# Reordered GpSimd work, one adding transfer fewer, and first products by two banks in a one-core decoder layer

## The chip, the core and the metric

The kernel runs on one core of a Trainium2 chip. The core has a matrix engine (TensorE; PE in the profile, with PEld for its weight loads), a vector engine (VectorE, DVE), a scalar engine (ScalarE, ACT), GpSimd (POOL), a queue engine that issues most loads (SyncE, SP), and 16 DMA engines. Each engine works off its own list of instructions in order; semaphores order the engines among each other. The metric is the device time of one execution in microseconds (us); less is better.

## What is computed

One layer of a decoder over 288 tokens (256 of a prompt, and 8 requests of 4 new tokens each), 2048 wide:

```python
def trunk_layer(x, hist_conv, hist_pool, pos0, norm1_g, w_in, b_in, conv_w, conv_b,
                ln_g, ln_b, pool_w, pool_scale, w_out, norm2_g, w_ff1, w_ff2):
    h = rmsnorm(x, norm1_g)
    proj = jnp.einsum("btd,de->bte", h, w_in) + b_in
    a, gate, z = proj[..., :D_CONV], proj[..., D_CONV:2 * D_CONV], proj[..., 2 * D_CONV:]
    u = a * jax.nn.sigmoid(gate)
    u_ext = jnp.concatenate([hist_conv, u], axis=1)
    c = jax.nn.silu(layernorm(depthwise_causal_conv(u_ext, conv_w, conv_b), ln_g, ln_b))
    z_ext = jnp.concatenate([hist_pool, z], axis=1)
    d = multiscale_pool(z_ext, pos0)
    p = jnp.einsum("btgc,gce->btge", d, pool_w).reshape(bsz, T, D_POOL) * pool_scale
    mix = jnp.concatenate([c, p], axis=-1)
    x = x + jnp.einsum("btm,md->btd", mix, w_out)
    h2 = rmsnorm(x, norm2_g)
    f = jnp.square(jax.nn.relu(jnp.einsum("btd,df->btf", h2, w_ff1)))
    x = x + jnp.einsum("btf,fd->btd", f, w_ff2)
    return x, u_ext[:, -(CONV_W - 1):], z_ext[:, -(POOL_MAX - 1):]
```

The depthwise convolution has 31 taps; the four pooling groups have windows of 2, 4, 8 and 16. All data are float32. The outputs are the normed x and the new histories.

## The kernel before

**Products in three parts.** A float32 product is made of fp32r ones. Each operand is split into a high half (hi, rounded) and a low half (lo, the rest): `whi`, `wlo` for weights, `hx`, `dx`, `mx`, `ax`, `fx` (each with both halves) for activations. A product is hi x hi, then wlo x hi, then whi x lo, so a pair of 128-row blocks k, k + 1 for one bank of 128 output columns takes six matmuls of 128 x 128 by 288 (`gemm`, all recorded as L291, their order is the list `todo`). A bank is an accumulator of TensorE; `bank2` hands out two of them, from a pool of two such pairs.

**Weights** come in blocks `wr` of 128 x 4 x 256 (512 KB), loaded by SP in the order of `weight_blocks` (two halves for each call of `load`). `split_part` makes `whi` on ScalarE (L260) and `wlo` in one of three ways. V: a subtraction raw - whi on VectorE (L265). G: two subtractions on GpSimd (L268). D: ScalarE writes -whi into `wlo` (L262), and a DMA that GpSimd issues (L263) adds the weights from memory to it; this is called an adding transfer. The table `WAYS` gives the way of each part by stage: "c3": "GDGG" are the four parts of the first loads of convolution pair 3.

**Order of stages.** `SEQUENCE` is c0 c1 c2 c3 c4 p3 c5 p2 P3 c6 p1 P2 p0 P1 c7 P0. c*i* projects the columns of a and gate of 128 convolution channels i (`conv_products`, two banks, 96 matmuls), p*g* those of pooling group g (`pool_group`), P*g* multiplies the pooled d of group g by `pool_w` (`pool_products`, 12 matmuls). p3.1 and so on below means part 1 of the four parts 0 to 3 of a stage's weights. Then w_out (`gemm` on `dx`, the pooled half, eight groups of two banks g = 0 to 7, each followed by an add into `xT` at L579), the layer norm over the convolution's output, w_out again (on `mx`, the convolution's half), and the two matrices of the MLP in a long loop.

**Convolution and pooling.** `conv_pair` multiplies a and gate by the row of norms (L432), builds u (L436), and runs 31 taps over the prompt on VectorE (L448, tile `pc`). For the 8 requests GpSimd multiplies history and taps into `prd` (L451; "history products"), which VectorE sums (L453). The taps are issued with a late priority (`later`), so that they fill what is left of VectorE's time. `pool_group` sums windows on GpSimd (L479 to L483), VectorE makes d of the prompt's columns (L484), and GpSimd d of the requests' columns (L486, L487; "pooling columns").

**TURN.** `classes` reorders the first matmuls of a gemm by the class (k + x) mod 2, where x is 0 for the high half of the activations and 1 for the low. Without it the classes alternate 0, 1, 0, 1; TURN is the string below. It stands at c2, c5, the first gemm of w_out, groups 5 and 7 of the pooled half of w_out, group 2 of its second half, and later in the MLP.

```python
TURN = "110100" * 4 + "01" * 6 + "1100" * 3
WAYS = {"c2": "GVGV", "c3": "GDGG", "c4": "GDGD", "p3": "GDDG", "c5": "GDGD", "c": "GGGV", "p": "GVVG", "w0": "VV", "w": "GG", "ff": "VV"}
```

A scheduler merges the engines' work by program order and priority; `tc.issue_after` forces an instruction behind another one.

## Time and profile before

| what | value |
|---|---|
| time, median of 3 runs | 1082.66 us (1081.39 to 1083.05) |
| the profiled execution's own time | 1082.43 us |
| its span | 1080.6 us |
| TensorE busy | 99% |
| VectorE, ScalarE, GpSimd busy | 59%, 44%, 16% |
| DMA | 190.71 MB, mean 176 GB/s |

The span is what the trace covers; the remaining 1.83 us of the execution lie around it. A row of the timeline gives start and length in us, engine, line, operation, the tiles (out<-in) and their shapes, a count, and in brackets what the first of them waited for. Rows of matmuls overlap, since they are pipelined: the distance of two starts is what a matmul costs. In the lists of waits stand who waited, for whom, the us in total, how often, and the longest. A row of windows has the window, its length, the busy time with the count of instructions, the granted clock, the DMA engines' busy share, and GB/s.

### The profile page before, as it was taken

How to read it: one execution, taken by the hardware profiler on the slowest of the kernel's cores; microseconds unless marked ns; L12 is line 12 of the kernel's file. 1: busy time of each engine (PE TensorE's matmuls, PEld its weight loads, DVE VectorE, ACT ScalarE, POOL GpSimd, SP SyncE). 2: the span in 40 equal slices, each digit the busy share in tenths (PEclk: the TensorE clock that was granted, in tenths of full speed). 3: DMA queues.
4: the chain of work that ended last, by engine and by line, in shares of the span. 5: the costliest groups of instructions: out<-in, count | busy, mean ns of one | idle time of the engine just before them, and what ended most of it. 6: DMA issues, size and time to landing. Idle time of an engine off the chain costs nothing.

```text
span 1080.6 us, 19528 instructions
## 1 busy us (share of the span) xinstructions
PE 1069.2 (99%) x8176; PEld 1067.9 (99%) x8176; DVE 633.7 (59%) x810; ACT 479.0 (44%) x588; POOL 175.9 (16%) x182
## 2 busy tenths in 40 slices
PE   9999999999999999999999999999999999999996
PEld 8999999999999999999999999999999999999996
DVE  7899999788654544444554444555544445554553
ACT  8654445665544433334443333444433334444441
POOL 0878979512000000000000000000000000000001
PEclk9999999999999999999999999999999999999999
DMA  9896478555555555555555555555555555555522
GB/s 326 288 263 182 145 187 247 177 171 173 162 173 166 169 175 163 170 173 165 170 174 164 170 170 167 171 173 162 173 168 167 173 171 164 173 166 170 172 79 88
DMA packets 58296, 190.71 MB, mean 176 GB/s; under 512 B 6240, under 2 KB 11232, under 8 KB 58208
## 3 DMA queue, kind: packets, MB, share of 16 engines
q1 hardware_dynamic: 56336, 184.35, 54.3%
q0 software_dynamic: 1008, 3.67, 1.9%
q8 instruction: 64, 1.05, 0.4%
q10 hardware_dynamic: 864, 1.44, 0.4%
q14 instruction: 24, 0.20, 0.0%
HBM read 185.16 MB, written 4.28 MB: 175 GB/s over the span
## 4 chain that ended last, share of the span: by engine, by line
PE 75%; issue 21%; ACT 2%; POOL 1%; DMA 1%; SPq 0%; POOLq 0%; DVE 0%
PE ac L291 74%; POOL wlo L268 1%; DMA wr<-in_w 1%; ACT whi L349 1%; PE pp L291 1%; DMA wlo<-in_w 1%; ACT hx L354 0%; ACT z_all L405 0%; POOL prd L451 0%; POOL xT L718 0%; ACT whi L260 0%; SPq L191 0%; POOLq L768 0%; DVE xT L691 0%; ACT whi L356 0%
## 5 line engine op out<-in xcount | busy, mean ns | idle before, releaser
L260 ACT CAST whi<-wr 128x1024 fp32r<-128x1024 f32 (+1 forms) x332 | 346.5, 1044 | 551.3 <-PE ac L291 536.7
L265 DVE TENSOR_TENSOR wlo<-wr,whi 128x1024 fp32r<-128x1024 f32 x288 | 353.5, 1227 | 348.1 <-ACT whi L260 348.1
L291 PE MATMUL ac<-ax,whi 128*128 128x288 f32 x2048 | 351.0, 292 | 0.0
L291 PE MATMUL ac<-fx,whi 128*128 128x288 f32 x2048 | 350.2, 292 | 0.0
L291 PEld LDWEIGHTS ac<-ax,whi 128*128 128x128 f32 x2048 | 296.0, 187 | 0.0
L291 PEld LDWEIGHTS ac<-fx,whi 128*128 128x128 f32 x2048 | 295.6, 187 | 0.0
L291 PE MATMUL ac<-ax,wlo 128*128 128x288 f32 x1024 | 217.3, 292 | 0.0
L291 PE MATMUL ac<-fx,wlo 128*128 128x288 f32 x1024 | 216.4, 292 | 0.0
L291 PEld LDWEIGHTS ac<-ax,wlo 128*128 128x128 f32 x1024 | 162.5, 187 | 0.0
L291 PEld LDWEIGHTS ac<-fx,wlo 128*128 128x128 f32 x1024 | 162.2, 187 | 0.0
L291 PE MATMUL ac<-hx,whi 128*128 128x288 f32 x768 | 131.9, 296 | 1.4 <-DVE hx L352 1.4
L718 POOL TENSOR_TENSOR xT<-xT,rf 128x288 f32<-128x288 f32 x4 | 3.1, 795 | 799.9 <-ACT rf L722 799.9
L291 PEld LDWEIGHTS ac<-hx,whi 128*128 128x128 f32 x768 | 112.6, 190 | 1.8 <-ACT hx L354 1.7
L268 POOL TENSOR_TENSOR wlo<-wr,whi 128x512 fp32r<-128x512 f32 x74 | 102.4, 1433 | 17.1 <-ACT whi L260 16.0
L448 DVE SCALAR_TENSOR_TENSOR pc<-u_all,vec,pc 128x256 f32<-128x256 f32 x232 | 99.3, 479 | 1.9 <-ACT pc L445 0.7
L291 PE MATMUL ac<-hx,wlo 128*128 128x288 f32 x384 | 80.4, 295 | 0.2 <-DMA wlo<-in_w 0.2
L291 PEld LDWEIGHTS ac<-hx,wlo 128*128 128x128 f32 x384 | 61.1, 189 | 0.4 <-DMA wlo<-in_w 0.4
L291 PE MATMUL ac<-dx,whi 128*128 128x288 f32 x256 | 46.8, 295 | 0.0
L291 PE MATMUL ac<-mx,whi 128*128 128x288 f32 x256 | 44.9, 293 | 0.0
L660 DVE SCALAR_TENSOR_TENSOR t<-ac,r 128x576 f32<-128x576 f32 x32 | 24.2, 757 | 25.4 <-PE ac L291 25.3
L291 PEld LDWEIGHTS ac<-dx,whi 128*128 128x128 f32 x256 | 38.4, 188 | 0.2
L291 PEld LDWEIGHTS ac<-mx,whi 128*128 128x128 f32 x256 | 37.5, 188 | 0.2 <-DVE xT L579 0.2
(129 smaller groups left out, 529.6 us busy)
## 6 DMA issues: line engine op xcount, KB each, us to landing
wr<-in_w SPq DMA_DIRECT2D x335, 512.0 KB, 3.8
wlo<-in_w POOLq DMA_DIRECT2D x7, 512.0 KB, 7.8
xT<-in_xT SPq DMA_DIRECT2D x8, 288.0 KB, 7.7
wr<-in_w SPq DMA_DIRECT2D x5, 256.0 KB, 3.9
out_u_out<-u_all SPq DMA_DIRECT2D x1, 1208.0 KB, 9.6
u_all<-in_hist_c SPq DMA_DIRECT2D x8, 136.0 KB, 5.3
out_z_out<-z_all SPq DMA_DIRECT2D x1, 668.0 KB, 9.2
z_all<-in_hist_p SPq DMA_DIRECT2D x4, 152.0 KB, 6.6
```

The lines of the kernel that those rows point to most:

```text
L260: nc.scalar.copy(hi, raw)
L265: nc.vector.tensor_tensor(lo, raw, f32(hi), op=ALU.subtract)
L268: nc.gpsimd.tensor_tensor(lo[:, j : j + 2, :], raw[:, j : j + 2, :], f32(hi[:, j : j + 2, :]), op=ALU.subtract)
L291: last = nc.tensor.matmul(*args, **kw)
L349: nc.scalar.copy(hi[:, blocks[0]], raw[:, blocks[0]])
L448: nc.vector.scalar_tensor_tensor(out=dst, in0=up[:, w : w + SEQ], scalar=cwv[:, w : w + 1], in1=pc, op0=ALU.mult, op1=ALU.add)
L660: nc.vector.scalar_tensor_tensor(out=t, in0=bk[:, :, :T], scalar=0.0, in1=both(rows2[0]), op0=ALU.max, op1=ALU.mult)
L718: eng.tensor_tensor(xk, xk, r[:, None, :].to_broadcast([P, n, T]), op=ALU.mult)
```

## The change

**Edits in words.** (1) `added` keeps the adding transfers; each `prd` is issued after one of them (L451, now L463), the taps of c2 and c3 wait in `waiting` for the next pair. (2) c4's second part is made by G instead of D: seven adding transfers become six. (3) In `pool_group` the pooling columns come ahead of VectorE's d, and `pooled` puts GpSimd's later subtractions behind them. (4) `load(order)` loads the second half of w_out's first blocks first, and `korder[k] ^ 4` takes it; of w0's two parts the first goes to GpSimd ("GV"). (5) P1's products stand at k = 8 of c7 instead of 12, P0's at matmul 24 of w_out's first gemm instead of 36, and that gemm's first 24 matmuls are sorted, whi ahead of wlo (`late`); its TURN begins at 24. (6) The first gemm of w_out's second half (`mixed`) takes its first k pairs 0 and 2 for the first two banks, then for the other two.

GpSimd's list from the first history products on. Names: `prd1` to `prd4` are the history products of c0 to c3; `wlo14` is c3.1, `wlo15` and `wlo16` are c3's other two, `wlo17` to `wlo20` are c4's four, `wlo21` to `wlo24` p3's four. Before:

```order
L451 TENSOR_TENSOR prd1_667<-u_all_87,vec_85 128x32x31
L451 TENSOR_TENSOR prd2_708<-u_all_87,vec_85 128x32x31
L263 DMA wlo14_609<-in_w 128x1024
L268 TENSOR_TENSOR wlo15_618<-wr15_613,whi15_617 128x512 x2
L268 TENSOR_TENSOR wlo16_623<-wr16_615,whi16_622 128x512 x2
L268 TENSOR_TENSOR wlo17_858<-wr17_853,whi17_857 128x512 x2
L451 TENSOR_TENSOR prd3_751<-u_all_87,vec_85 128x32x31
L263 DMA wlo18_863<-in_w 128x1024
L268 TENSOR_TENSOR wlo19_872<-wr19_867,whi19_871 128x512 x2
L263 DMA wlo20_877<-in_w 128x1024
L268 TENSOR_TENSOR wlo21_1027<-wr21_1022,whi21_1026 128x512 x2
L451 TENSOR_TENSOR prd4_918<-u_all_87,vec_85 128x32x31
```

and after the change:

```order
L263 DMA wlo14_609<-in_w 128x1024
L463 TENSOR_TENSOR prd1_667<-u_all_87,vec_85 128x32x31
L463 TENSOR_TENSOR prd2_708<-u_all_87,vec_85 128x32x31
L269 TENSOR_TENSOR wlo15_618<-wr15_613,whi15_617 128x512 x2
L269 TENSOR_TENSOR wlo16_623<-wr16_615,whi16_622 128x512 x2
L269 TENSOR_TENSOR wlo17_822<-wr17_817,whi17_821 128x512 x2
L269 TENSOR_TENSOR wlo18_827<-wr18_819,whi18_826 128x512 x2
L269 TENSOR_TENSOR wlo19_836<-wr19_831,whi19_835 128x512 x2
L263 DMA wlo20_841<-in_w 128x1024
L463 TENSOR_TENSOR prd3_883<-u_all_87,vec_85 128x32x31
L269 TENSOR_TENSOR wlo21_990<-wr21_985,whi21_989 128x512 x2
L263 DMA wlo22_995<-in_w 128x1024
```

The adding transfer of c3 now stands ahead of `prd1` and `prd2`, c4's `wlo18` is a pair of subtractions and no longer an adding transfer, `prd3` has moved from ahead of `wlo18` to behind `wlo20`, and `prd4` no longer stands ahead of `wlo22`.

GpSimd's list at pooling groups 1 (`s9`, `d3`) and 0 (`s10`, `d4`). Before:

```order
L479 TENSOR_TENSOR s9_1865<-s8_1862 128x420 x2
L268 TENSOR_TENSOR wlo48_2045<-wr48_2040,whi48_2044 128x512 x2
L268 TENSOR_TENSOR wlo49_2050<-wr49_2042,whi49_2049 128x512 x2
L483 TENSOR_TENSOR s9_1865<-s9_1865,rcnt_131 128x2x3
L268 TENSOR_TENSOR wlo50_2059<-wr50_2054,whi50_2058 128x512 x2
L486 TENSOR_SCALAR s9_1865<-s9_1865 128x2x8x4
L479 TENSOR_TENSOR s10_2029<-z_all_91 128x422 x2
L487 TENSOR_TENSOR d3_1868<-s9_1865,z_all_91 128x2x32
L483 TENSOR_TENSOR s10_2029<-s10_2029,rcnt_131 128x2
```

and after the change:

```order
L491 TENSOR_TENSOR s9_1865<-s8_1862 128x420 x2
L495 TENSOR_TENSOR s9_1865<-s9_1865,rcnt_131 128x2x3
L497 TENSOR_SCALAR s9_1865<-s9_1865 128x2x8x4
L498 TENSOR_TENSOR d3_1868<-s9_1865,z_all_91 128x2x32
L269 TENSOR_TENSOR wlo48_2045<-wr48_2040,whi48_2044 128x512 x2
L269 TENSOR_TENSOR wlo49_2050<-wr49_2042,whi49_2049 128x512 x2
L269 TENSOR_TENSOR wlo50_2059<-wr50_2054,whi50_2058 128x512 x2
L491 TENSOR_TENSOR s10_2029<-z_all_91 128x422 x2
L495 TENSOR_TENSOR s10_2029<-s10_2029,rcnt_131 128x2
```

The three rows on `s9` and `d3` at L495 to L498 stand together, ahead of the subtractions of `wlo48`, `wlo49` and `wlo50`, where L483, L486 and L487 were spread among them.

TensorE's list where w_out's second half begins (`ac22` holds the first two banks, `ac23` the other two; `mx1` and `mx2` are the first two pairs of blocks). Before:

```order
L291 MATMUL ac22_2841<-mx1_2816,whi69_2741 128x288 x2
L291 MATMUL ac22_2841<-mx1_2816,wlo69_2742 128x288 x2
L291 MATMUL ac22_2841<-mx1_2816,whi69_2741 128x288 x4
L291 MATMUL ac22_2841<-mx1_2816,wlo69_2742 128x288 x2
L291 MATMUL ac22_2841<-mx1_2816,whi69_2741 128x288 x2
L291 MATMUL ac23_2842<-mx1_2816,whi71_2803 128x288 x2
L291 MATMUL ac23_2842<-mx1_2816,wlo71_2804 128x288 x2
L291 MATMUL ac23_2842<-mx1_2816,whi71_2803 128x288 x4
L291 MATMUL ac23_2842<-mx1_2816,wlo71_2804 128x288 x2
L291 MATMUL ac23_2842<-mx1_2816,whi71_2803 128x288 x2
```

and after the change:

```order
L292 MATMUL ac22_2842<-mx1_2817,whi69_2742 128x288 x2
L292 MATMUL ac22_2842<-mx1_2817,wlo69_2743 128x288 x2
L292 MATMUL ac22_2842<-mx1_2817,whi69_2742 128x288 x4
L292 MATMUL ac22_2842<-mx1_2817,wlo69_2743 128x288 x2
L292 MATMUL ac22_2842<-mx1_2817,whi69_2742 128x288 x2
L292 MATMUL ac22_2842<-mx2_2824,whi69_2742 128x288 x2
L292 MATMUL ac22_2842<-mx2_2824,wlo69_2743 128x288 x2
L292 MATMUL ac22_2842<-mx2_2824,whi69_2742 128x288 x4
L292 MATMUL ac22_2842<-mx2_2824,wlo69_2743 128x288 x2
L292 MATMUL ac22_2842<-mx2_2824,whi69_2742 128x288 x2
L292 MATMUL ac23_2843<-mx1_2817,whi71_2804 128x288 x2
```

The first matmul into `ac23` stands behind 24 others instead of 12, and `mx2` is first read behind 12 instead of 24.

The diff:

```diff
--- before.py
+++ after.py
@@ -70,7 +70,7 @@
 TURN = "110100" * 4 + "01" * 6 + "1100" * 3
 
 
-WAYS = {"c2": "GVGV", "c3": "GDGG", "c4": "GDGD", "p3": "GDDG", "c5": "GDGD", "c": "GGGV", "p": "GVVG", "w0": "VV", "w": "GG", "ff": "VV"}
+WAYS = {"c2": "GVGV", "c3": "GDGG", "c4": "GGGD", "p3": "GDDG", "c5": "GDGD", "c": "GGGV", "p": "GVVG", "w0": "GV", "w": "GG", "ff": "VV"}
 
 
 VEC = (("norm1_g", 16), ("b_in", 24), ("conv_b", 8), ("ln_g", 8), ("ln_b", 8), ("pool_scale", 8), ("norm2_g", 16), ("norm_f", 16))
@@ -161,10 +161,10 @@
 
     blocks = iter(range(5, io["w"].shape[0]))
 
-    def load():
+    def load(order=(0, 1)):
 
         src, raw = io["w"][next(blocks)], []
-        for h in range(2):
+        for h in order:
             raw.append((raw_tile(), src[:, 4 * h : 4 * h + 4, :]))
             nc.sync.dma_start(*raw[-1])
         return raw
@@ -249,7 +249,7 @@
         last = mm(psum[:, 0, :T], minus, total, start=True, stop=True)
         return row_of(psum, psum[:, 0, :T], *args), last
 
-    turns = {}
+    turns, added, newest, pooled = {}, [], {}, []
 
     def split_part(raw, src, hi, lo, way):
 
@@ -260,12 +260,13 @@
         nc.scalar.copy(hi, raw)
         if way == "D":
             nc.scalar.activation(lo, f32(hi), AF.Copy, scale=-1.0)
-            nc.gpsimd.dma_start(lo, src, accum_op=ALU.add)
+            added.append(nc.gpsimd.dma_start(lo, src, accum_op=ALU.add))
         elif way == "V":
             nc.vector.tensor_tensor(lo, raw, f32(hi), op=ALU.subtract)
         else:
             for j in range(0, raw.shape[1], 2):
-                nc.gpsimd.tensor_tensor(lo[:, j : j + 2, :], raw[:, j : j + 2, :], f32(hi[:, j : j + 2, :]), op=ALU.subtract)
+                with tc.issue_after(pooled[-1].ins) if pooled else nullcontext():
+                    nc.gpsimd.tensor_tensor(lo[:, j : j + 2, :], raw[:, j : j + 2, :], f32(hi[:, j : j + 2, :]), op=ALU.subtract)
 
     def spl():
         return [wspl.tile([P, 4, 256], F32R, name=nm("w" + part), tag="w" + part) for part in ("hi", "lo")]
@@ -293,7 +294,7 @@
             chain[0] = last.ins
         return last
 
-    def gemm(banks, rhs, m_outer=False, between={}, classes="", by_part=False, gets=None, pairs=None):
+    def gemm(banks, rhs, m_outer=False, between={}, classes="", by_part=False, gets=None, pairs=None, late=0):
 
 
         n = len(rhs)
@@ -314,6 +315,7 @@
             for k, m in pairs:
                 begins[len(todo)] = (k, m) if m else k
                 todo += [(k + d, m, w, x) for d, w, x in ((0, 0, 0), (1, 0, 0), (0, 1, 0), (1, 1, 0), (1, 0, 1), (0, 0, 1))]
+        todo[:late] = sorted(todo[:late], key=lambda p: p[2])
         head = todo[: len(classes)]
         for j, c in enumerate(classes):
             todo[j] = next(p for p in head if c == "." or (p[0] + p[3]) % 2 == int(c))
@@ -381,8 +383,8 @@
         for kind, i in SEQUENCE[2:]:
             yield [pool_weights(i)] if kind == "P" else [split(load(), f"{kind}{i}") for _ in range(2)]
         for j in range(8):
-            get = split(load(), f"w{j}")
-            yield [lambda k, m, get=get: get(korder[k], m)]
+            get = split(load((1, 0)), f"w{j}")
+            yield [lambda k, m, get=get: get(korder[k] ^ 4, m)]
         for _ in range(8):
             yield [split(load())]
         for _ in range(2 * DFF // 256):
@@ -412,7 +414,7 @@
     rb = row("rb")
 
 
-    cs, pcs = [], []
+    cs, pcs, waiting = [], [], []
     sum_c = tmpp.tile([P, 2, T], F32, name="sum_c", tag="ag2", bufs=2)
 
     def history(i):
@@ -436,6 +438,15 @@
             nc.vector.scalar_tensor_tensor(out=out, in0=a, scalar=v("b_in", i), in1=b, op0=ALU.add, op1=ALU.mult)
         if i % 2 == 0:
             cs.append(actp.tile([P, 2, T], F32, name=nm("c"), tag="c", bufs=4))
+        while waiting:
+            taps(*waiting.pop())
+        if i in (2, 3):
+            waiting.append((i, up, us))
+        else:
+            taps(i, up, us)
+
+    def taps(i, up, us):
+
         c = cs[i // 2][:, i % 2, :]
         with later():
             if i % 2 == 0:
@@ -448,7 +459,8 @@
                 nc.vector.scalar_tensor_tensor(out=dst, in0=up[:, w : w + SEQ], scalar=cwv[:, w : w + 1], in1=pc, op0=ALU.mult, op1=ALU.add)
             prd = prdp.tile([P, NB, NS, CW + 1], F32, name=nm("prd"), tag="prd")
             nc.scalar.activation(prd[:, :, :, CW], ones[:, 0 : NB * NS].rearrange("p (b t) -> p b t", t=NS), AF.Identity, bias=v("conv_b", i), scale=0.0)
-            nc.gpsimd.tensor_tensor(prd[:, :, :, 0:CW], windows(us, CW), cwv[:, None, None, :].to_broadcast([P, NB, NS, CW]), op=ALU.mult)
+            with tc.issue_after(added[max(0, min(2, i - 1))].ins):
+                nc.gpsimd.tensor_tensor(prd[:, :, :, 0:CW], windows(us, CW), cwv[:, None, None, :].to_broadcast([P, NB, NS, CW]), op=ALU.mult)
             cso = c[:, SEQ:T]
             nc.vector.tensor_reduce(samples(cso, NS), prd, axis=AX.X, op=ALU.add)
             if i % 2 and 1 < i < N8 - 1:
@@ -481,10 +493,11 @@
         d = tmpp.tile([P, 2, T], F32, name=nm("d"), tag="ag2", bufs=2)
         first_sums = s[:, :, PH : PH + w - 1]
         nc.gpsimd.tensor_tensor(first_sums, first_sums, rcnt[:, None, w - 2 : 2 * w - 3].to_broadcast([P, 2, w - 1]), op=ALU.mult)
-        nc.vector.scalar_tensor_tensor(out=d[:, :, 0:SEQ], in0=s[:, :, PH:ZO], scalar=1.0 / w, in1=z[:, :, PH:ZO], op0=ALU.mult, op1=ALU.subtract)
         news = [x[:, :, ZO:ZL].rearrange("p m (b t) -> p m b t", t=ZS)[:, :, :, PH:] for x in (s, z)]
         nc.gpsimd.tensor_scalar(news[0], news[0], 1.0 / w, None, op0=ALU.mult)
-        nc.gpsimd.tensor_tensor(d[:, :, SEQ:T].rearrange("p m (b t) -> p m b t", t=NS), news[0], news[1], op=ALU.subtract)
+        last = nc.gpsimd.tensor_tensor(d[:, :, SEQ:T].rearrange("p m (b t) -> p m b t", t=NS), news[0], news[1], op=ALU.subtract)
+        newest[g] = last
+        nc.vector.scalar_tensor_tensor(out=d[:, :, 0:SEQ], in0=s[:, :, PH:ZO], scalar=1.0 / w, in1=z[:, :, PH:ZO], op0=ALU.mult, op1=ALU.subtract)
         dh, dl = act2("dx", tag="p", bufs=4)
         nc.scalar.copy(dh, d)
         nc.vector.tensor_tensor(dl, d, f32(dh), op=ALU.subtract)
@@ -525,18 +538,23 @@
     for kind, i in SEQUENCE[3:-1]:
         if (kind, i) == ("P", 1):
             continue
+        if i == 7:
+            pooled.append(newest[1])
         if kind == "c":
-            conv_pair(i, conv_products(i, classes=TURN if i == 5 else "", **(dict(gets=ahead(1), between={12: lambda: pool_products(1)}) if i == 7 else {})))
+            conv_pair(i, conv_products(i, classes=TURN if i == 5 else "", **(dict(gets=ahead(1), between={8: lambda: pool_products(1)}) if i == 7 else {})))
         elif kind == "p":
             pool_group(i)
         else:
             pool_products(i)
+    pooled.append(newest[0])
     proj = [halves(dd[k // 2])[k % 2] for k in korder]
     bks = [bank2() for _ in range(2)]
     both_gets = [ahead(1) for _ in range(2)]
     early = [(k, m) for k in (0, 2, 4) for m in range(4)]
     early.sort(key=lambda km: km[1] // 2)
-    gemm(each(bks[0]) + each(bks[1]), proj, gets=[lambda k, m: both_gets[m // 2][0](k, m % 2)], between={(0, 2): lambda: pool_products(0)}, classes="." * 36 + TURN, pairs=early + [(6, m) for m in range(4)])
+    mixed = [(k, m) for k in range(0, KT // 2, 2) for m in range(4)]
+    mixed.sort(key=lambda km: (km[0] // 4, km[1] // 2) if km[0] < 4 else (1, 0))
+    gemm(each(bks[0]) + each(bks[1]), proj, gets=[lambda k, m: both_gets[m // 2][0](k, m % 2)], late=24, between={4: lambda: pool_products(0)}, classes="." * 24 + TURN, pairs=early + [(6, m) for m in range(4)])
     chain.clear()
     load_table(AF.Abs_reciprocal_sqrt, f32(mixp[1][0])[:, 0:1])
     with later(2 * LATER):
@@ -596,7 +614,7 @@
     chain.append(last)
     bks = [bank2() for _ in range(2)]
     two_gets = [ahead(0) for _ in range(2)]
-    gemm(each(bks[0]) + each(bks[1]), mixc, gets=[lambda k, m: two_gets[m // 2][0](k, m % 2)])
+    gemm(each(bks[0]) + each(bks[1]), mixc, gets=[lambda k, m: two_gets[m // 2][0](k, m % 2)], pairs=mixed)
     chain.clear()
     for g in range(8):
         bk = bks[g] if g < 2 else bank2()
```

## The prediction

> **What bounds the kernel now.** I read the page's table of engines first, then the list of what PE waits for, the chain of waits, PE's timeline around each wait, and last the counts of matmuls in equal windows.
>
> ```profile
> PE 1069.2 (99%) x8176; PEld 1067.9 (99%) x8176; DVE 633.7 (59%) x810; ACT 479.0 (44%) x588; POOL 175.9 (16%) x182
> ```
>
> TensorE is the bound: 99% of the span, and no matmul is added or removed. Only what keeps matmuls from following each other at their shortest distance can go. The chain of waits shows one such place:
>
> ```profile
> 42.27 2.14 POOL prd L451
> 44.41 5.97 DMA wlo<-in_w
> 50.38 0.04 issue
> ```
>
> An adding transfer (a weight part's low half, way D) was queued behind a history product (prd) on GpSimd, and landed at 50.38. PE's timeline there:
>
> ```profile
> 48.77 0.68 PE L291 MATMUL ac<-hx,whi 128*128 128x288 f32 x4
> 49.29 0.42 PE L291 MATMUL ac<-hx,wlo 128*128 128x288 f32 x2
> 49.55 0.68 PE L291 MATMUL ac<-hx,whi 128*128 128x288 f32 x4
> 50.42 0.54 PE L291 MATMUL ac<-hx,wlo 128*128 128x288 f32 x2 [0.20 <-DMA wlo<-in_w]
> 50.80 0.69 PE L291 MATMUL ac<-hx,whi 128*128 128x288 f32 x4
> ...
> 51.59 0.70 PE L291 MATMUL ac<-hx,whi 128*128 128x288 f32 x4
> 52.12 0.43 PE L291 MATMUL ac<-hx,wlo 128*128 128x288 f32 x2
> 52.39 0.70 PE L291 MATMUL ac<-hx,whi 128*128 128x288 f32 x4
> ```
>
> Starts count here, since matmuls overlap. From 48.77 to 49.55 six matmuls take 0.78 us, 130 ns each. From 49.55 to 50.80 six take 1.25: the wait costs 0.47, more than the 0.20 in the bracket. And behind it six take 0.80 (51.59 to 52.39), 133.3 ns each. Equal windows show how long that lasts:
>
> ```profile
> 51.00:85.00 34.00, 34.00 (x257) 1.00 0.94 255
> 93.00:127.00 34.00, 34.00 (x263) 1.00 0.51 160
> 178.00:192.00 14.00, 14.00 (x110) 1.00 0.75 230
> 220.00:231.00 11.00, 11.00 (x85) 1.00 0.56 175
> ```
>
> Columns: window, length, PE busy (matmuls), granted clock, DMA share, GB/s. In the same 34 us there are 6 matmuls fewer than later at the same clock. The slow pace holds until c5's first matmuls at 85, which stand in the order TURN; 93 to 127 is quick again. It is not the DMA traffic: 178 to 192 is quick at 230 GB/s (110 in 14.00), and 220 to 231 is slow at 175. That second slow stretch also starts with a wait and ends with a TURN (that of group g = 2 of the second half of w_out):
>
> ```profile
> 218.93 0.42 PE L291 MATMUL ac<-mx,wlo 128*128 128x288 f32 x2
> 219.19 0.90 PE L291 MATMUL ac<-mx,whi 128*128 128x288 f32 x4
> 219.93 0.43 PE L291 MATMUL ac<-mx,wlo 128*128 128x288 f32 x2
> ```
>
> ```profile
> 218.75 0.74 DVE L579 TENSOR_TENSOR xT<-xT,ac 128x576 f32<-128x576 f32 x1
> ```
>
> ```profile
> L291 PEld LDWEIGHTS ac<-mx,whi 128*128 128x128 f32 x256 | 37.5, 188 | 0.2 <-DVE xT L579 0.2
> ```
>
> Six matmuls take 1.00, so 0.22 is lost. The matmul that is late is the thirteenth of this gemm, the first into its second pair of banks, and VectorE empties those banks until 218.75 + 0.74 = 219.49; the page has the weight load's wait. So I read: a wait in a stream puts the matmuls out of step, each then costs 3.3 ns more, until a TURN puts them back.
>
> **What the change removes.** (1) Wait at 50: 0.47. (2) Slow pace from 50.8 to 85: 257 matmuls in the window less the two that overlap its edge, 255 x 3.33 ns = 0.85. (3) Wait at 219.4: 0.22. (4) Slow pace to 231: (85 - 2) x 3.33 ns = 0.28. Sum 1.82 us, **1.8**.
>
> For (1), the transfer moves ahead of both prd on GpSimd:
>
> ```profile
> 40.16 4.33 POOL L451 TENSOR_TENSOR prd<-u_all,vec 128x992 f32<-128x992 f32 x2
> 44.41 1.01 POOL L263 DMA_DIRECT2D wlo<-in_w  x1
> 45.21 7.75 POOL L268 TENSOR_TENSOR wlo<-wr,whi 128x512 fp32r<-128x512 f32 x6
> ...
> 63.76 2.16 POOL L451 TENSOR_TENSOR prd<-u_all,vec 128x992 f32<-128x992 f32 x1
> ```
>
> ```profile
> 39.26 1.06 ACT L262 ACTIVATE wlo<-whi 128x1024 fp32r<-128x1024 f32 x1
> ...
> 63.30 1.05 ACT L260 CAST whi<-wr 128x1024 fp32r<-128x1024 f32 x1 [1.10 <-PE ac L291]
> 64.38 1.06 ACT L262 ACTIVATE wlo<-whi 128x1024 fp32r<-128x1024 f32 x1
> ...
> 67.54 1.06 ACT L262 ACTIVATE wlo<-whi 128x1024 fp32r<-128x1024 f32 x1
> ```
>
> ```profile
> DMA to landing us min/median/max: 6.0/7.8/10.2
> ```
>
> Its input (the negation on ScalarE) is ready at 39.26 + 1.06 = 40.32, so it starts 4.1 us earlier and has until 49.55 + 4 x 0.13 = 50.07: 9.7 us. This very transfer took 5.97; the slowest of the seven took 10.2, at full DMA load. I take 6 to 9, so it is in time. Next in line for c3 are GpSimd's subtractions, which started at 45.21 behind all three and still do. The two prd come about 1 us later (the issue ahead of them); VectorE's sums over them wait, and behind those only taps and c3's own multiply, whose bank PE wants back some 10 us later.
>
> For (2), no later transfer may be late either. The tight ones are those of p3, which PE reads here:
>
> ```profile
> 76.12 0.43 PE L291 MATMUL ac<-hx,wlo 128*128 128x288 f32 x2
> ...
> 79.32 0.43 PE L291 MATMUL ac<-hx,wlo 128*128 128x288 f32 x2
> ```
>
> PE comes there earlier by 0.47 and by 0.02 for each 0.80 since 50.8: at 75.0 and 78.1. The first can leave GpSimd at 64.38 + 1.06 = 65.44, since the prd that ended at 63.76 + 2.16 = 65.92 ahead of it now stands behind it; the second at 67.54 + 1.06 = 68.60. That leaves 9.6 and 9.5 us if ScalarE is no earlier, and about 1.1 more if it is: its cast at 63.30 waited for PE, so I take 10.4. Against that stands at most 10.2. One of c4's transfers ahead of them is gone, though (512 KB, at the 255 GB/s of the first window 2.0 us of traffic), so I expect 8 to 10 and no wait.
>
> The Trainium skill, "DMA: Bandwidth & Descriptors", section "Anatomy of one DMA — SWDGE (gpsimd) path", gives 2.0 us plus the bytes over 436 GB/s, an estimate of 3.2 us for these 512 KB. By it no transfer could be late even before; the trace has 6.0 to 10.2, so it doesn't bear this out and the rows decide.
>
> **What it adds.** c4's second part goes to GpSimd: two subtractions, at 7.75 / 6 = 1.29 each, for one issue of 1.0 and ScalarE's negation of 1.06. Ten subtractions now stand in a row, so c2's prd comes some 5 us later, and c3's (2.2 us) ends near 68. VectorE's sums over both stood at 67.22; behind the second are two taps and the multiply of the next pair, which waited for PE:
>
> ```profile
> 72.86 0.47 DVE L432 TENSOR_TENSOR ac<-ac,rb 128x288 f32<-128x288 f32 x1 [0.95 <-PE ac L291]
> ```
>
> That wait takes up to 0.95 us of lateness. Cost 0; the bound is 2.6 us of GpSimd above, and 1.0 of issue below (a gain), and I take 0, nearest to that row.
>
> One part of w0 goes from VectorE to GpSimd (2.6 us there). Its low half is first read by the 17th matmul instead of the 3rd, since the first 24 are sorted: 14 x 0.13 = 1.8 us more time. Cost 0.
>
> GpSimd's pooling columns go ahead of subtractions, VectorE's d behind them:
>
> ```profile
> DVE d L484 <- POOL s L483: 1.2, 2, 1.0
> DVE tz L470 <- PE ac L291: 0.9, 1, 0.9
> ```
>
> ```profile
> 128.83 0.38 POOL L486 TENSOR_SCALAR s<-s 128x64 f32<-128x64 f32 x1 [0.81 <-DVE d L484]
> ```
>
> This takes 1.2 us of waiting from VectorE and delays a subtraction by about 1 us (0.38, its neighbours and no wait). VectorE needs that gain: its first add into xT is what g = 2 waits for.
>
> ```profile
> 178.11 0.74 DVE L579 TENSOR_TENSOR xT<-xT,ac 128x576 f32<-128x576 f32 x1
> ```
>
> ```profile
> 178.97 0.68 PE L291 MATMUL ac<-dx,whi 128*128 128x288 f32 x4
> ```
>
> The third of these four (179.23) is g = 2's first: 0.38 us behind the add's end at 178.85. PE will be 1.32 earlier, so the add must be 0.94 earlier; 1.2 from d, and up to 0.9 more from the wait for PE, cover it.
>
> P1's products come 24 matmuls earlier, P0's 12, and the loads of w_out's first halves are swapped: the same matmuls in another order, with the pooling results ready earlier by the wait that went: 0. For (3), the second banks are first needed at index 24 instead of 12, 1.56 us later, against 0.22 missing. The second pair of mx comes forward instead, its low half read at index 16.
>
> **Sum.** The profiled execution took 1082.43 us (span 1080.6 and 1.83 around it), 0.23 under the median of 1082.66. 1082.43 - 1.8 = 1080.6 for it; against the median **1080.8**.
>
> **Rivals.** (A) *An adding transfer stays late*: c3's at 9.8 us or more would keep 0.47 + 0.85, leaving 1082.1. One of p3's at over 10.4 waits 0.1 to 1 us, then 68 matmuls at 3.33 ns to 85 add 0.23: 1081.1 to 1082.1. For it: 10.2 was measured. Against: less traffic, earlier issue. Chance 0.11.
>
> (B) *The change doesn't do what it says to the pace*: waits go, 133.3 ns stays for another reason. Gain 0.47 + 0.22 = 0.69, so 1082.0. For it: I have no row that shows why the pace changes. Against: both slow stretches start at a wait and end at a TURN. Chance 0.07.
>
> (C) *Another wait takes its place*: VectorE's add at 178 late by 0.1 to 0.5, then slow to the TURN of g = 5, three groups of 48 matmuls x 3.33 ns = 0.48; or mx's second low half late at 219. 1081.2 to 1081.8. Chance 0.09.
>
> (D) *Slower*: GpSimd falls behind after c5's TURN, where a wait costs its own length and the slow pace up to the next TURN, that of w_out's first products near 165.
>
> ```profile
> 131.76 4.13 POOL L268 TENSOR_TENSOR wlo<-wr,whi 128x512 fp32r<-128x512 f32 x2
> ...
> 145.50 5.05 POOL L268 TENSOR_TENSOR wlo<-wr,whi 128x512 fp32r<-128x512 f32 x4
> ```
>
> A subtraction takes 1.26 at best (5.05 / 4) and up to 2.07. Ten at 2.07 are 8 us late. A wait at 100 costs (165 - 100) / 0.13 x 3.33 ns = 1.67 by pace alone, so it decides from a wait of 0.15 us (there all the gain is gone), and over 0.2% from about 2.3 us: 1083 to 1085. Against it: GpSimd idles 2.5 us ahead of 138 in the timeline, and the queue at c4 catches up before 85. Chance 0.05.
>
> The Trainium skill, "SBUF — State Buffer", section "Who interferes with whom", says that a VectorE instruction with two inputs in SBUF contends with a GpSimd instruction that reads SBUF; that is a reason to fear for work moved onto GpSimd. The spread of 1.26 to 2.07 agrees with it as far as it goes; by that rule the time would be that of (D), without it the forecast.
>
> **How the numbers follow.** Forecast 0.68, A 0.11, B 0.07, C 0.09, D 0.05. What a measurement of this kernel can tell from no change is about 0.2%, 2.2 us: below 1080.5 is faster, above 1084.8 slower. The forecast stands 0.3 inside "same"; the three runs before span 1.66 us, so about 0.4 of its 0.68 falls below: 0.27 faster. D gives 0.04 slower. Same: 0.69. The range: 1.1 below the forecast for the spread of runs, and above to take in A, B and C: 1079.7 to 1082.4.
>
> **What would show it.** Right: no PE wait for a wlo transfer, 263 matmuls in 51 to 85 (moved by half a microsecond), 87 in 220 to 231, a span of 1078.8, the first adding transfer issued near 40.4. Wrong: a bracket with DMA wlo at 75 to 79 (A), 257 in the window without a wait ahead of it (B), a wait for xT at 178 (C), or a wait for POOL wlo between 92 and 165 (D).

## The result, and the profile after

| | median | runs |
|---|---|---|
| before | 1082.02 us | 8 (1081.39 to 1083.05) |
| changed | 1085.88 us | 8 (1084.85 to 1086.32) |

The ratio is 1.0033 (95% interval 1.0023 to 1.0043): slower, where 1.8 us less was forecast. The profiled execution of the changed kernel took 1085.71 us, its span 1083.9 (before 1080.6). Line numbers have moved: L291 is L292, L436 is L438, L448 is L459, L484 is L500, L490 is L503, L502 is L515, L579 is L597. All waits of TensorE in the changed kernel:

```profile
PE pp L292 <- DVE dx L515: 1.8, 1, 1.8
PE ac L292 <- DVE u_all L438: 1.6, 1, 1.6
PE ac L292 <- DVE hx L354: 1.3, 1, 1.3
PE warm L214 <- DVE cst L231: 1.0, 1, 1.0
PE ac L292 <- DVE xT L597: 0.5, 1, 0.5
```

The wait for an adding transfer is gone, three waits for VectorE are new. The windows of the prediction:

```profile
51.00:85.00 34.00, 34.00 (x264) 1.00 0.90 254
93.00:127.00 34.00, 34.00 (x263) 1.00 0.49 152
178.00:192.00 14.00, 13.54 (x103) 1.00 0.77 216
220.00:231.00 11.00, 11.00 (x86) 1.00 0.55 179
```

264 matmuls where 257 were: the slow pace to 85 is gone, as is the wait ahead of it; the waits list has nothing at 219 either. But 178 to 192 has 7 fewer than before (110): a wait of 0.5 and a new slow pace behind it. The loss begins at w_out's first products. TensorE's timeline there (`pp` is P0's bank):

```profile
165.87 1.20 PE L292 MATMUL ac<-dx,wlo 128*128 128x288 f32 x8
168.84 0.53 PE L292 MATMUL pp<-dx,whi 128*128 128x288 f32 x2 [1.76 <-DVE dx L515]
...
171.98 0.29 PE L292 MATMUL ac<-dx,whi 128*128 128x288 f32 x1
173.87 0.37 PE L292 MATMUL ac<-dx,whi 128*128 128x288 f32 x1 [1.59 <-DVE u_all L438]
```

From 165.87 eight matmuls take 1.04, and the next starts at 168.84: 1.93 lost. From 171.98 to 173.87 another 1.76. With 0.9 in the third window that is 4.6; the rest is the slow pace around them, on to g = 5. The sum can be checked by the starts of the same matmul in both kernels: the 1201st starts at 164.06 before and at 162.75 now, 1.31 earlier; the 1501st, behind g = 5, at 203.44 and 207.22, 3.78 later; the 1801st, behind the second slow stretch, at 243.43 and 246.73, 3.3 later. So 5.1 was lost between 164 and 207, and 1.31 + 0.48 = 1.8 was gained on either side of it.

What VectorE did there, in the changed kernel and, last two rows, what GpSimd did:

```profile
161.74 1.33 DVE L500 SCALAR_TENSOR_TENSOR d<-s,z_all 128x512 f32<-128x512 f32 x1
...
166.51 1.45 DVE L503 TENSOR_TENSOR dx<-d,dx 128x576 fp32r<-128x576 f32 x1
...
168.28 0.50 DVE L515 SCALAR_TENSOR_TENSOR dx<-pp,vec,dx 128x288 fp32r<-128x288 f32 x1
...
173.08 0.64 DVE L438 SCALAR_TENSOR_TENSOR u_all<-ac,vec,tg 128x256 f32<-128x256 f32 x2
```

```profile
161.23 1.29 POOL L269 TENSOR_TENSOR wlo<-wr,whi 128x512 fp32r<-128x512 f32 x1
...
165.83 1.51 POOL L269 TENSOR_TENSOR wlo<-wr,whi 128x512 fp32r<-128x512 f32 x1 [1.60 <-ACT whi L260]
```

The same instructions before, VectorE and then TensorE:

```profile
165.42 0.74 DVE L490 TENSOR_TENSOR dx<-d,dx 128x576 fp32r<-128x576 f32 x1
...
167.24 0.50 DVE L502 SCALAR_TENSOR_TENSOR dx<-pp,vec,dx 128x288 fp32r<-128x288 f32 x1
...
170.37 0.63 DVE L436 SCALAR_TENSOR_TENSOR u_all<-ac,vec,tg 128x256 f32<-128x256 f32 x2
```

```profile
169.78 0.42 PE L291 MATMUL pp<-dx,whi 128*128 128x288 f32 x2
...
171.34 0.29 PE L291 MATMUL ac<-dx,whi 128*128 128x288 f32 x1
```

P0's products need the one bank `pp`, which VectorE frees with the second scaling of P1's result, at 167.74 before, 2.04 ahead of need. TensorE's first matmul into the second pair of banks at 171.34 needs c7's banks, freed at 171.00, 0.34 ahead. In the changed kernel VectorE ends these at 168.78 and 173.72, later by 1.0 and 2.7, while TensorE comes earlier.

And dx took 1.45 where it took 0.74: GpSimd's subtraction began at 165.83 and ended at 167.34, dx began between and ended 0.62 behind it. A list of VectorE's instructions with two inputs in the on-chip memory, 60 to 172 us (count, busy, mean ns), before and then changed:

```profile
L265 DVE TENSOR_TENSOR wlo<-wr,whi 128x1024 fp32r<-128x1024 f32 x10 | 13.6, 1364 | 0.4 <-ACT whi L260 0.4
L490 DVE TENSOR_TENSOR dx<-d,dx 128x576 fp32r<-128x576 f32 x4 | 4.3, 1068 | 0.0
L484 DVE SCALAR_TENSOR_TENSOR d<-s,z_all 128x512 f32<-128x512 f32 x4 | 3.4, 855 | 1.2 <-POOL s L483 1.2
L265 DVE TENSOR_TENSOR wlo<-wr,whi 128x512 fp32r<-128x512 f32 x4 | 3.3, 818 | 0.0
```

```profile
L265 DVE TENSOR_TENSOR wlo<-wr,whi 128x1024 fp32r<-128x1024 f32 x9 | 14.3, 1594 | 0.4 <-ACT whi L260 0.4
L500 DVE SCALAR_TENSOR_TENSOR d<-s,z_all 128x512 f32<-128x512 f32 x4 | 5.0, 1255 | 1.5 <-POOL s L497 1.5
L265 DVE TENSOR_TENSOR wlo<-wr,whi 128x512 fp32r<-128x512 f32 x4 | 4.3, 1072 | 0.0
L503 DVE TENSOR_TENSOR dx<-d,dx 128x576 fp32r<-128x576 f32 x4 | 4.1, 1019 | 0.0
```

24.6 us for 22 instructions before, 27.7 for 21 after, though one subtraction of 1.2 went to GpSimd. That is 4.3 us more of stretch. The taps, whose second input lies in a bank (`pc`), kept their 478 ns in both kernels:

```profile
L448 DVE SCALAR_TENSOR_TENSOR pc<-u_all,vec,pc 128x256 f32<-128x256 f32 x164 | 69.1, 478 | 0.4
L459 DVE SCALAR_TENSOR_TENSOR pc<-u_all,vec,pc 128x256 f32<-128x256 f32 x161 | 67.5, 478 | 0.8 <-ACT pc L456 0.7
```

VectorE's windows from 60 to the moment when c7's banks are free, before and then changed (length, busy time, count):

```profile
60.00:171.00 111.00, 107.19 (x225) 1.00 0.69 197
60.00:173.72 113.72, 110.08 (x225) 1.00 0.67 192
```

The same number of instructions, 2.9 us more of busy time, and 3.6 us of idle time where 3.8 was: VectorE is late by the lengths of its instructions, not by their number or by waits. **Theory:** VectorE's instructions with both inputs in the on-chip memory stand still while GpSimd works, and TensorE waits for VectorE. **Rivals:** P0 was moved too far forward; VectorE's list is wrongly ordered; one part of the change (pooling order, w0) is the culprit.

### The profile page after: what moved, and what is told of

Read it like the earlier page. It is cut to its first block, busy times and chain, and to the rows that moved or that the text cites. A ratio compares the mean times of both kernels' runs of the same rounds, so it can differ in the third digit from the quotient of the medians.

```text
span 1083.9 us, 19534 instructions
## 1 busy us (share of the span) xinstructions
PE 1069.0 (99%) x8176; PEld 1067.4 (98%) x8176; DVE 637.1 (59%) x809; ACT 477.5 (44%) x587; POOL 181.5 (17%) x185
## 4 chain that ended last, share of the span: by engine, by line
PE 70%; issue 21%; DVE 5%; POOL 4%; DMA 0%; ACT 0%; POOLq 0%
PE ac L292 69%; DVE pc L459 3%; POOL wlo L269 2%; POOL s L491 1%; DVE wlo L265 1%; DVE d L500 0%; DMA wr<-in_w 0%; DVE dx L503 0%; DVE c L465 0%; POOL xT L736 0%; POOL prd L463 0%; DVE dx L515 0%; DVE ac L434 0%; DVE u_all L438 0%; PE norm L292 0%
## 5 line engine op out<-in xcount | busy, mean ns | idle before, releaser
L292 PE MATMUL ac<-ax,whi 128*128 128x288 f32 x2048 | 351.0, 292 | 0.0
L292 PE MATMUL ac<-fx,whi 128*128 128x288 f32 x2048 | 350.1, 292 | 0.0
L292 PEld LDWEIGHTS ac<-ax,whi 128*128 128x128 f32 x2048 | 296.0, 187 | 0.0
L292 PEld LDWEIGHTS ac<-fx,whi 128*128 128x128 f32 x2048 | 295.5, 187 | 0.0
L292 PE MATMUL ac<-ax,wlo 128*128 128x288 f32 x1024 | 217.3, 292 | 0.0
L292 PE MATMUL ac<-fx,wlo 128*128 128x288 f32 x1024 | 216.3, 292 | 0.0
L292 PEld LDWEIGHTS ac<-ax,wlo 128*128 128x128 f32 x1024 | 162.6, 187 | 0.0
L292 PEld LDWEIGHTS ac<-fx,wlo 128*128 128x128 f32 x1024 | 162.2, 187 | 0.0
L292 PE MATMUL ac<-hx,whi 128*128 128x288 f32 x768 | 131.4, 295 | 1.3 <-DVE hx L354 1.3
L292 PEld LDWEIGHTS ac<-hx,whi 128*128 128x128 f32 x768 | 112.0, 190 | 1.7 <-ACT hx L356 1.6
L269 POOL TENSOR_TENSOR wlo<-wr,whi 128x512 fp32r<-128x512 f32 x78 | 108.4, 1453 | 18.1 <-ACT whi L260 15.5
L459 DVE SCALAR_TENSOR_TENSOR pc<-u_all,vec,pc 128x256 f32<-128x256 f32 x232 | 99.5, 481 | 2.5 <-ACT pc L456 1.4
L292 PE MATMUL ac<-hx,wlo 128*128 128x288 f32 x384 | 80.1, 294 | 0.0
L292 PEld LDWEIGHTS ac<-hx,wlo 128*128 128x128 f32 x384 | 61.0, 190 | 0.0
L292 PE MATMUL ac<-dx,whi 128*128 128x288 f32 x256 | 47.0, 297 | 2.0 <-DVE u_all L438 1.6
L292 PE MATMUL ac<-mx,whi 128*128 128x288 f32 x256 | 44.5, 292 | 0.0
L292 PEld LDWEIGHTS ac<-dx,whi 128*128 128x128 f32 x256 | 38.5, 188 | 2.6 <-issue 1.8
L292 PEld LDWEIGHTS ac<-mx,whi 128*128 128x128 f32 x256 | 37.4, 187 | 0.0
```

What stands on the lines that cost most here:

```text
L269: nc.gpsimd.tensor_tensor(lo[:, j : j + 2, :], raw[:, j : j + 2, :], f32(hi[:, j : j + 2, :]), op=ALU.subtract)
L292: last = nc.tensor.matmul(*args, **kw)
L459: nc.vector.scalar_tensor_tensor(out=dst, in0=up[:, w : w + SEQ], scalar=cwv[:, w : w + 1], in1=pc, op0=ALU.mult, op1=ALU.add)
```

## Experiments

**One part undone at a time.** Each starts from the changed kernel. First, d goes ahead of the pooling columns again and the subtractions aren't held:

```diff
+        nc.vector.scalar_tensor_tensor(out=d[:, :, 0:SEQ], in0=s[:, :, PH:ZO], ...)
         news = [x[:, :, ZO:ZL]...]
-            pooled.append(newest[1])
-    pooled.append(newest[0])
```

> The changed kernel with VectorE's d ahead of the pooling columns again and GpSimd's subtractions no longer held behind them. Theory (the pooling order makes VectorE's d and dx start right behind a GpSimd subtraction and stretch; that is some 2 of the 4.5 us that VectorE lost): VectorE frees c7's banks 1.5 to 2.5 us earlier and the time falls to 1083 to 1084.5. Rival (the stretched instructions come from chance phases, not from this order): the time stays within 0.5 us of the changed kernel, 1085.4 to 1086.4.

1087.32 us (1087.0 to 1087.79): slower still. A wait of 3.4 us for dx stands at a pooling product in its trace. So undoing the pooling order alone gives nothing back: with P1's products at their earlier place, which this run keeps, the new order helps by 1.4.

```diff
-between={8: lambda: pool_products(1)}  /  late=24, between={4: ...}, classes="." * 24 + TURN
+between={12: lambda: pool_products(1)} /  between={(0, 2): ...}, classes="." * 36 + TURN
```

> The changed kernel with P1's products at k = 12 of c7 and P0's behind 36 matmuls of w_out's first gemm again, and no sorting of its first 24. Theory (VectorE's lateness sets the end of the wait, whatever the order in front of c7's banks): the wait at P0 goes, but the one for c7's banks grows by as much; time within 0.6 us of the changed kernel. Rival (P0's earlier place is the loss): the wait of 1.8 us at P0 goes and nothing grows, 1083.5 to 1084.

1085.96 us, unchanged, as the theory said. Its mechanism came out otherwise: the wait at P0 went, but the one for c7's banks went too, and in their place TensorE waits for P1's results, 1.4 for ScalarE's half and 0.8 for VectorE's, and behind that 0.9 for P0's. Where the waits stand depends on the order in front; the time hardly does, so the earlier places of P1 and P0 didn't make the loss.

```diff
-"w0": "GV"  get = split(load((1, 0)), ...)  get(korder[k] ^ 4, m)
+"w0": "VV"  get = split(load(), ...)        get(korder[k], m)
```

> The changed kernel with both parts of w0 on VectorE and w_out's blocks loaded in the old order. Theory (GpSimd's two subtractions for w0 stretch VectorE's dx by 0.65 and spare it 1.2 us of its own): VectorE is 0.5 us later at c7's banks and the time rises by 0.3 to 0.8 us, to 1086.2 to 1086.7. Rival (work moved onto GpSimd costs VectorE more than it spares): the time falls by 0.5 us or more.

1083.98 us (1082.84 to 1084.9), 1.9 less, or 1.4 by the ratios to the kernel before (1.0020, 1.0012 to 1.0029, against 1.0033). My expectation was wrong and its rival right: two subtractions moved onto GpSimd cost VectorE as much as the one it was spared, or more. In this trace its 22 instructions take 27.6 us, where 21 took 27.7. The run also puts back the order of w_out's loads, which isn't separated from w0's part.

**Parts alone, on the kernel before.** Edits (1), (2) and (6) of the change only:

> Keeps of the change only the order of adding transfers, history products and taps, c4's part on GpSimd, and the first gemm of w_out's second half by two banks; the pooling columns, w0's part with its load order, and the places of P1 and P0 are as before. Theory (the four terms of the prediction are right, and the loss is a new wait at w_out's first products that the other parts make): no wait at 50 or 219, none at 164 to 180, 1.8 us under the kernel before, about 1080.2. Rival (the earlier PE alone runs into VectorE, which frees c7's banks only 0.34 us ahead of need): PE is 1.3 us earlier there, so a wait of about 1 us plus slow pace of 0.5 us remains, and the time is about 1081.7.

1083.7 us (1082.46 to 1085.63), ratio 1.0018 (1.0009 to 1.0027). The wait at 50 is gone, yet the kernel is slower: the rival's direction, and 2 us more than it said. With w0 undone alone the time was 1083.98, so the pooling order and the places of P1 and P0 together add next to nothing to these parts. The trace shows the stretch with the old pooling order and w0 on VectorE: the same 22 instructions as before take 28.6 us in place of 24.6. One of them, a dx, started 0.22 us behind GpSimd's history product:

```profile
128.81 2.22 POOL L463 TENSOR_TENSOR prd<-u_all,vec 128x992 f32<-128x992 f32 x1 [1.25 <-DVE u_all L438]
```

```profile
129.03 2.62 DVE L503 TENSOR_TENSOR dx<-d,dx 128x576 fp32r<-128x576 f32 x1
```

2.62 for 0.74: it ends 0.62 behind GpSimd's end at 131.03, as above. Two adding transfers landed late as well, at 73.89 and 77.50 (0.14 and 0.32 lost, and the slow pace behind), but the larger loss, 3.1, lies between 157 and 178. The same parts without the taps held and without (6):

```diff
-with tc.issue_after(added[max(0, min(2, i - 1))].ins):
+with tc.issue_after(added[max(0, min(2, i - 1, len(added) - 1))].ins):
-        if i in (2, 3):
+        if i in ():
```

> The kernel before with only the order of adding transfers and history products and c4's part on GpSimd; the taps of c2 and c3 don't wait for the next pair, and the second half of w_out is as before. Theory (TensorE's 1.3 us of gain shift the phase between VectorE and GpSimd, whatever the taps): waits of 1 to 2.5 us between 92 and 172 again, 1082.5 to 1084.5. Rival (the held taps make VectorE late): no such wait beyond 0.4 us, 1080.8 to 1081.4.

1085.06 us, above the theory's range: the waits for VectorE are there again (1.6 us in all), so the taps aren't the cause. In this trace two adding transfers were late too (0.7 us in all, at 68 and 79), the prediction's rival (A), with the slow pace behind them. Edit (6) by itself:

> The kernel before with one edit alone: the first gemm of w_out's second half takes its first pairs by two banks. Theory (this part of the prediction is right by itself): no wait at 219.4, no slow pace to 231, 0.49 us less, 1081.4 to 1081.6 where the kernel before gives 1081.9. Rival (the wait returns for the second mx pair): no gain, 1081.9.

1081.63 against 1081.95, ratio 0.9996 (0.9987 to 1.0005). The wait at 219 isn't in its trace, and TensorE gains 0.48 there, from the 1501st matmul to the 1801st; by the times the gain can't be told from none.

**GpSimd's subtractions left out.** This is the direct test, on both kernels, from p2's weights on. ScalarE writes -whi in place of each pair, and the weights are not added, so these two kernels leave out a part of the layer's arithmetic:

```diff
-"c": "GGGV", "p": "GVVG", "w0": "GV", "w": "GG"
+"c": "AAAV", "p": "AVVA", "w0": "AV", "w": "AA"
+        elif way == "A":
+            nc.scalar.activation(lo, f32(hi), AF.Copy, scale=-1.0)
```

> The changed kernel with GpSimd's weight subtractions from p2 on (way G of stages c6, c7, p2, p1, p0, w0 and w) left out: ScalarE writes the negated high half in their place, and the raw weights are not added. Nothing else on GpSimd or VectorE changes. Theory (VectorE is late because its instructions with two inputs stand still while GpSimd's subtractions run): VectorE's subtractions, d and dx take their shortest times (1.21, 0.68, 0.74), some 6 us less up to 170, the waits at P0 and at c7's banks go, and the time is about 1080 to 1081. Rival (VectorE's list is simply too long there, or the order is wrong): its times shrink little and the waits of 1.8 and 1.6 us stay, 1085 to 1086.

> The kernel before with GpSimd's weight subtractions from p2 on (way G of c6, c7, p2, p1, p0 and w) left out in the same way: ScalarE writes the negated high half in their place, and the raw weights are not added. Theory (the kernel before doesn't wait for VectorE, so its time doesn't depend on them): the waits at 50 and 219 with the slow paces stay, 1081.5 to 1082.3, and the changed kernel without them is 1.2 to 1.8 us faster than this. Rival (the subtractions cost the kernel before as much): 1081 or less, and the gain seen without them was not the change's.

Changed: 1080.69 us (1079.42 to 1081.6), ratio to the kernel before 0.9989 (0.9980 to 0.9998), as the theory said. Before: 1082.54 (1081.53 to 1084.08), 1.0010 (1.0001 to 1.0020). The two were measured on different chips, so that the medians' difference of 1.85 us comes so near to the prediction's 1.8 is luck. By the kernel before on each chip, the changed kernel gains 1.3 without the subtractions and the kernel before loses 1.0, a distance of about 2.2; the latter has a loss of its own in its trace, 0.23 at 175 and the slow pace behind it, 0.75 in all. The trace says more than the medians. Of the changed kernel without subtractions the 241st matmul starts at 37.20, 0.61 earlier than before, and the 1801st at 241.01, 2.42 earlier: 1.81 gained between, at the two places of the prediction, and nothing lost. VectorE's groups there (its lines stand two further on):

```profile
L267 DVE TENSOR_TENSOR wlo<-wr,whi 128x1024 fp32r<-128x1024 f32 x9 | 12.0, 1329 | 0.4 <-ACT whi L260 0.2
...
L267 DVE TENSOR_TENSOR wlo<-wr,whi 128x512 fp32r<-128x512 f32 x4 | 3.4, 847 | 0.3 <-ACT whi L260 0.3
...
L505 DVE TENSOR_TENSOR dx<-d,dx 128x576 fp32r<-128x576 f32 x4 | 3.0, 754 | 0.2
L502 DVE SCALAR_TENSOR_TENSOR d<-s,z_all 128x512 f32<-128x512 f32 x4 | 2.7, 681 | 0.0
```

```profile
166.93 0.64 DVE L440 SCALAR_TENSOR_TENSOR u_all<-ac,vec,tg 128x256 f32<-128x256 f32 x2 [0.51 <-ACT tg L438]
```

21.1 us in place of 27.7, and c7's banks are free at 167.57 instead of 173.72. Of these 6.1 us 0.6 are the earlier start seen at 37; the rest is busy time, since VectorE idles from 60 on for 4.0 us in all, where it was 3.6:

```profile
60.00:167.57 107.57, 103.59 (x223) 1.00 0.70 205
```

No new wait is left in TensorE's list.

**VectorE's list reordered.** The last ten taps of c6 wait for c7's u:

```diff
+        if i == 7:
+            taps(*held, first=HELD, hold=last.ins)
+        elif i == 6:
+            held.extend((i, up, us))
+            taps(i, up, us, last=HELD)
```

> The changed kernel with the last ten taps of c6 (and what follows them) issued behind c7's product u, so that VectorE frees c7's banks some 5 us earlier; the work is the same. Theory (what counts is how long VectorE's list in front of P1's results and c7's banks takes): the waits at P0 and c7's banks and the one at g = 2 go, 5 us less than the changed kernel, 1080.5 to 1081.3. Rival (the held taps are needed soon after, for the mean over channels or for the next adds into xT): part of it returns as a wait between 178 and 200, 1082 to 1085.

1086.15 us. c7's banks came free only 1.0 earlier (172.74), two transfers were late by 0.8, and 1.2 returned as a wait for the mean over channels, as the rival said; the time lies above both ranges. It settles nothing on the order of VectorE's list.

**Adding transfers in place of the subtractions.** These kernels compute the whole layer. The edit of the first:

```diff
-"c": "GGGV", "p": "GVVG", "w0": "GV"
+"c": "DDDV", "p": "DVVD", "w0": "DV"
```

> The changed kernel with way D in place of G for c6, c7, p2, p1, p0 and w0: ScalarE's negation and an adding transfer take the place of GpSimd's two subtractions, with the right result; VectorE's own parts stay. Theory (GpSimd's subtractions hold up VectorE's instructions with two inputs; DMA has room there, a share near 0.5): VectorE's d, dx and subtractions shrink by 4 to 6 us up to 170, the waits at P0, c7's banks and g = 2 go, 1080.0 to 1081.0. Rival (13 more transfers of 512 KB are late in their turn, or GpSimd's issues and ScalarE's negations come late): a new wait for DMA wlo between 92 and 165 with the slow pace behind it, 1082 to 1085.

> As the run before it, and VectorE's parts of these stages by way D too, so that VectorE has some 9 us less to do up to 170. Theory: VectorE had enough room already, so nothing is gained over that run, within 0.4 us of it. Rival (VectorE's list is still what P0 and c7's banks wait for): another 0.5 us or more faster; or twice the transfers are late: slower by 1 us or more.

> The first run's kernel (order of adding transfers, c4's part, second half of w_out by two banks; pooling columns, w0 and places of P1 and P0 as before) with way D in place of G for c6, c7, p2, p1 and p0. Theory (the order of the pooling columns and P1's and P0's places are worth nothing once VectorE isn't held up): within 0.5 us of the changed kernel with these transfers, 1080.0 to 1081.0. Rival (those parts are needed to meet w_out's first products): 1 us or more slower than it.

> The kernel before with the second half of w_out by two banks and way D in place of G for c6, c7, p2, p1 and p0; the order of adding transfers is as before. Theory (the wait at 50 with its slow pace stays, 1.3 us, the one at 219 goes): 1081.2 to 1081.7. Rival (holding up VectorE cost the kernel before something too): 1080.8 or less.

1091.32, 1096.05, 1090.58 and 1091.15 us. The transfers were late on whatever base, the rival of the first two runs; in the last two neither theory nor rival had such a time. So none of the four tells what VectorE would gain. TensorE's wait and the transfers' times in the first of them:

```profile
PE ac L292 <- DMA wlo<-in_w: 5.5, 2, 2.9
```

```profile
DMA to landing us min/median/max: 6.6/8.7/10.5
```

My cover, "DMA has room, a share near 0.5", was wrong: between 90 and 165 us the share rose from 0.52 (150 GB/s) to 0.93 (234 GB/s). Nor was VectorE left in peace there (last section).

**Two parts only.** p0's two middle parts were VectorE's longest subtractions of 128 x 1024 (2.28 and 2.22 us) in the changed kernel. By adding transfers, on the changed kernel, without w0's part, and on the kernel of parts (1), (2), (6):

```diff
+"p0": "GDDG"
```

> The changed kernel with the two middle parts of p0 by adding transfers in place of VectorE's subtractions (2.28 and 2.22 us there). Theory: VectorE is some 3.5 us earlier at P1's results and c7's banks, most of the waits of 1.8 and 1.6 us go, 1082 to 1083.5. Rival (these transfers are late at p0's products): a wait for DMA wlo near 140 with the slow pace behind it, 1085 or more.

> The same with both parts of w0 on VectorE and w_out's blocks loaded in the old order. Theory: 1081 to 1082.5, 1 us or more faster than the run before it, since w0's subtractions on GpSimd no longer stretch dx. Rival (late transfers): 1084 or more.

> The first run's kernel (order of adding transfers, c4's part, second half of w_out by two banks) with p0's two middle parts by adding transfers. Theory: the wait for P1's results goes, 1081 to 1082.5. Rival (late transfers): 1084 or more.

1084.77, 1084.56 and 1085.54 us, slower than the theory's ranges. The waits at P0, c7's banks and g = 2 are gone from all three traces, which the theory asked, but the price came with it (first of the three):

```profile
PE ac L292 <- DMA wlo<-in_w: 2.1, 1, 2.1
```

So the same two parts went to GpSimd, in its idle time, without a transfer:

```diff
+"p0": "GGGG"
```

> The changed kernel with all four parts of p0 on GpSimd. Theory: VectorE is 3 us earlier at P1's results and c7's banks, no transfer can be late, GpSimd fills its idle 2.8 us and is 2 us later behind; the waits at P0, c7's banks and g = 2 mostly go, 1081 to 1083. Rival (GpSimd is now late with p0's and c7's parts, or its longer run of subtractions stretches VectorE's d and dx as much as it spared): a wait for POOL wlo between 135 and 165, or the old waits, 1085 or more.

> The same with both parts of w0 on VectorE and w_out's blocks loaded in the old order (the fourth run's kernel with p0 on GpSimd). Theory: as before, and w0's subtractions don't stretch dx: 1080.5 to 1082.5. Rival: GpSimd late, 1084 or more.

1083.24 us (1082.02 to 1086.28), ratio 1.0017 (1.0009 to 1.0026), just above the theory's range; and with w0 on VectorE 1081.70 (1080.41 to 1086.05), ratio 1.0003 (0.9993 to 1.0013), within it. The last takes back nearly all that the change lost (ratio 1.0033) and equals the kernel before. It agrees with VectorE's time there being what decides; VectorE is spared two subtractions in these runs, not only stretch. No version that computes the whole layer was clearly faster than the kernel before.

## Why the prediction was wrong

1. *The four terms removed.* Right, place by place: the waits at 50 and 219 and both slow paces are gone, 1.31 and 0.48 in the changed kernel's trace and 1.81 with GpSimd's subtractions out of the way, where 1.8 was added up. A wait started the slow pace again (178 to 192 in the changed kernel). It need not be long: in the kernel before without GpSimd's subtractions six matmuls at 50 took 0.86 (from 49.29 to 50.15), a loss of 0.08, and 51 to 85 has 257 matmuls all the same. Why it does is still not shown.
2. *"VectorE needs that gain ... 1.2 from d, and up to 0.9 more ... cover it."* This is the step that failed. I let VectorE be earlier by 1.2 to 2.1; it was 2.7 later at c7's banks, and the add itself began at 181.62 in place of 178.11. Part of the gain never came. The wait for PE fell from 0.9 to 0.3, but d waited for GpSimd longer than before, 1.5 for 1.2, now for the pooling columns that had been put ahead of it:

```profile
DVE d L500 <- POOL s L497: 1.5, 1, 1.5
DVE tz L482 <- PE ac L292: 0.3, 1, 0.3
```

The larger part is that its durations were taken as fixed, while some 20 of its instructions depend on when GpSimd runs. Parts (1), (2) and (6) alone stretched them by 4.0 (24.6 to 28.6). They make TensorE 1.3 us earlier, which moves VectorE's instructions against GpSimd's, but they also change GpSimd's own list; which of the two does it is not shown. Moving w0's part to GpSimd (with its order of loads), a term that I put at 0, cost 1.4 to 1.9.
3. *"P1's products come 24 matmuls earlier, P0's 12 ...: 0."* Wrong as a sum. I checked one place where TensorE meets VectorE, the add at 178, and not the two ahead of it. P0 moves forward by 1.32 + 1.56 = 2.88 with 2.04 to spare; c7's banks had 0.34 to spare for a TensorE that is 1.3 earlier. So by an estimate from these slacks even a VectorE on its old times would have taken back about a microsecond: 0.84 at P0, and 0.14 at c7's banks, for a TensorE that is then 0.48 earlier. With P0 at its old place all of it, 1.32 less 0.34, would stand at c7's banks.
4. *Rival (D)* had the sign and GpSimd's contention, but on the wrong side: it priced late GpSimd subtractions, and the trace has no wait for POOL wlo. The section quoted with it says more than I used. The Trainium skill, "SBUF — State Buffer", section "Who interferes with whom", has the order of issue decide which of the two blocks. The traces agree: dx at 166.51 in the changed kernel, begun while a GpSimd subtraction ran, ended 0.62 after it. In the kernel before, VectorE's subtraction at 163.00 began first and took 1.28, near its shortest 1.21, and GpSimd's beside it lost. The second of GpSimd's pair lost to dx at 165.42, which took its shortest time (the two starts are 0.02 apart, too near to tell which came first). The pair took 3.62 us where two subtractions at 1.26, the shortest, take 2.5:

```profile
163.00 1.28 DVE L265 TENSOR_TENSOR wlo<-wr,whi 128x1024 fp32r<-128x1024 f32 x1
...
163.70 3.62 POOL L268 TENSOR_TENSOR wlo<-wr,whi 128x512 fp32r<-128x512 f32 x2 [0.49 <-ACT whi L260]
```
5. *Rival (C)* came true as written: the add into xT is late by 0.5 at g = 2, and the slow pace up to g = 5 costs another 0.5. But it is the smallest of the three waits; the 3.7 us ahead of it, at P0 and at c7's banks, were in no rival.
6. *Rival (A)*, late adding transfers at p3: not in the changed kernel's profile, but in several variants, 0.3 to 0.8 us. The margin was as thin as stated.
7. The range ended at 1082.4. It took in wait lengths at GpSimd, DMA and the pace, and no change in VectorE's durations.
